# One PSUM pool for both stages of the odd mixer, the projections taking turns in the second stage's banks

## The chip, the cores and the metric

The kernel runs on one core of one Trainium2 chip. A core has several engines, each with an instruction queue of its own: TensorE (PE) for matmuls and transposes, VectorE (DVE), ScalarE (ACT) and GpSimd (POOL) for everything elementwise, and SyncE (SP), which here only issues DMAs. Matmuls write to PSUM, which has eight banks of 128 x 512 float32. The metric is the device time of one execution in microseconds (us); a smaller number is better.

## The reference

The program is a diffusion trunk of two layers over 256 latent and 256 context tokens, 1024 wide, in float32. Each layer is a mixer, modulated by a conditioning vector (adaLN), and then a mixture of 32 experts. The change is in the mixer of the second ("odd") layer, which joins a bidirectional gated DeltaNet (GDN, 4 heads of 128) with multi-head latent attention (MLA, 8 heads). Cut to what matters:

```
h = modulate(rms_norm(x), shift, scale)          # 512 tokens x 1024
q, k, v, z, tail = split(h @ odd_w_in)            # 4 x 512 columns, and 432: gates, MLA q rank 256, kv rank 128, rope 32
q, k, v = silu(short_conv5(.))                    # 5 taps along the tokens
q, k = l2_norm(q), l2_norm(k)
beta = sigmoid(tail[0:8]);  log_a = -exp(a_log) * softplus(tail[8:16] + dt_bias)
# GDN, in chunks, forward and backward in time:
T = strict_lower(beta * (k k^T) * gamma) + I      # gamma: decays from cumsum(log_a)
u, w = solve(T, beta v), solve(T, beta k exp(g))
o, S = scan over chunks of (u - w S, ...)
# MLA: q from rms_norm(cq) @ wq_up, k and v from rms_norm(ckv) @ wkv_up, rope, softmax attention
y = concat(rms_norm(o) * silu(z), attention) @ odd_w_out
x = x + gate * y;  x = x + gate2 * experts(modulate(rms_norm(x)))
```

The vectors shift, scale and gate come from silu(c) @ ada_w + ada_b, called "ada" in the kernel; it is computed in pieces of 2048 columns that are slipped in between other work.

## The kernel before, in words

The order of the instructions on each engine is not the order of the source. The odd mixer is built under a scheduler that has its own model of how long things take, and that emits on each engine what it thinks can start first; which buffers a pool has is part of what it sees, so a change of a pool can reorder every queue. The experts behind it have a hand-written PE order.

`odd_mixer` (L1341 to L1579) has two stages, each with a PSUM pool of its own, and the second pool opens when the first has closed.

Stage 1, pool `odps`: 4 banks named acc, 2 named mx, 2 named g. It normalises and transposes the tokens (L792); projects k (`proj_T`, the three matmuls L128 to L130 of a product of numbers split in a high and a low half); runs the 5-tap convolution of k on DVE (L1477, 4 taps by 4 heads) with, for each head, column sums of squares (L1485) and k k^T (L1494) on PE; projects the 432 tail columns (`tail_proj`, four banks, one for 128 tokens each: g, g, acc, acc); makes the gates, the decays (`gdn_decays`, L1586 on DVE, L1588 on PE, an Exp on ACT at L1591) and the matrices Ball (L1456, 32 multiplications on DVE); solves the 32 x 32 diagonal blocks on DVE (`gdn_solve`, L1630 to L1659); projects q, z and v; and, only after the solve (`issue_after`), convolves q and v on DVE (L1477 again), with the sums for q (L1485, copied to rq by L1487). The tail's MLA ranks are normed (L1337) and transposed (L1433, L1437), k is transposed to rows (L1507, into k_tok) and v too (L1500, into v_tok).

Stage 2, pool `gdps`: 2 banks named at, 3 mx, 2 mx2, 1 po. Inverses by doubling (`gdn_inverse`, L1672 to L1688) for the chunks 2 and 3 run interleaved with MLA's up projections (L1855) and their norms; then the second ada group (called ada2 here: L700 into po, copied to ada_r at L703, written to DRAM by L707 and read back as f1A by L734), which needs nine pieces of weights (one of them the bias row); then the chunks 0 and 1, the scans and the attention.

Weights come in by SP through five buffers named w (L110). Before each projection a piece of w is split: ACT writes the high half wh (L120) and DVE the low half wl (L121), with two buffers of each. SP issues in order; an SP instruction that waits for a buffer holds up the ones behind it.

Of the kernel before, what the change touches and what calls it, by code (L numbers as in the profile page):

```python
# [58 lines left out]
class Trunk:  # L59
# [1280 lines left out]
    def odd_mixer(self, ada, x_sb, x_done, S):  # L1340
# [23 lines left out]
        hp = xst.enter_context(tc.tile_pool(reuse_waits="tile", name="odh", bufs=1, side="right"))  # L1364
        psum = xst.enter_context(tc.tile_pool(reuse_waits="tile", name="odps", bufs=1, space=PSUM))
        hT = [hp.tile([128, 8, 512], F32R, name=f"hT{i}") for i in range(2)]
        with tc.tile_pool(reuse_waits="tile", name="odx", bufs=1) as xp:
            chunk = self.norm_T([x_sb[:, t] for t in range(NT)], hT, xp, lambda i: psum.tile(
                [128, 2, 256], F32, name="mx" if i in (4, 5) else "acc", bufs=2 if i in (4, 5) else 4),
                lambda c2: self.mods[1], 7)  # L1370
            for c2 in range(4):
                chunk(c2)
# [4 lines left out]
        cw = pool.tile([128, 12, 5], F32, name="cw")  # L1377
        pc = psum.tile([128, 12, 8], F32, name="mx", bufs=2)
        for a in range(12):
# [14 lines left out]

        def acc():
            return psum.tile([128, 512], F32, name="acc", bufs=4)

        dec = pool.tile([128, 2, NT, 4], F32, name="dec")
        tl = pool.tile([128, NT, 432], F32, name="tl")

        def tail_proj():
            names = iter(("g", "g", "acc", "acc"))

            def bank():
                n = next(names)
                return psum.tile([128, 512], F32, name=n, bufs=2 if n == "g" else 4)

            pa = self.proj_blocks(hT, S["tail"], range(NT), bank, 432)
            for t in range(NT):
                nc.scalar.activation(tl[:, t], pa[t][:, 0:432], AF.Copy)  # L1410
# [16 lines left out]
        def tail():  # L1427
            nc.vector.tensor_copy(kr, tl[:, :, 400:432])
            for t in range(NT):
                ps = tl[:, t]  # L1430
                ck = self.rms_rows(ps[:, 272:400], kvnw, 128, pool, "ckn")
                pt = psum.tile([128, 4, 128], F32, name="mx", bufs=2)
                nc.tensor.transpose(pt[:, 0], ck, self.ident)  # L1433
                if t < 2:
                    cq = self.rms_rows(ps[:, 16:272], qnw, 256, pool, "cqn")
                    for c in range(2):
                        nc.tensor.transpose(pt[:, 1 + c], cq[:, c * 128:(c + 1) * 128], self.ident)  # L1437
                    nc.scalar.activation(cqT[:, :, t * 128:(t + 1) * 128], pt[:, 1:3], AF.Copy)
                nc.scalar.activation(ckvT[:, t * 128:(t + 1) * 128], pt[:, 0], AF.Copy)
# [19 lines left out]
        def conv(kind, w0, pa):  # L1459
# [3 lines left out]
            for h in range(4):  # L1463
# [16 lines left out]
                if kind != "v":  # L1480
                    sq = raw.rearrange("p a b -> p (a b)")
                    nc.scalar.activation(sq, s, AF.Square)
                    ss = psum.tile([128, 4], F32, name="mx", bufs=2)[:, :nt]
                    for t in range(nt):
# [5 lines left out]
                    nc.vector.tensor_scalar_add(r, ss, 1e-6)  # L1490
                    kk = psum.tile([128, 4, 128], F32, name="mx", bufs=2)
                    for t in range(4):
# [4 lines left out]
                    continue  # L1497
                pt = psum.tile([128, 4, 128], F32, name="mx", bufs=2)
                for t in range(nt):
# [3 lines left out]
        def k_rows():  # L1503
            for h in range(4):
                pt = psum.tile([128, 4, 128], F32, name="mx", bufs=2)
                for t in range(4):
                    nc.tensor.transpose(pt[:, t], kT[:, h, t * 128:(t + 1) * 128], self.ident)  # L1507
                nc.scalar.activation(k_tok[:, :, h], pt, AF.Copy)
# [29 lines left out]
        gst.close()  # L1538
        with tc.tile_pool(reuse_waits="tile", name="gd2", bufs=1, side="right") as p2, tc.tile_pool(reuse_waits="tile", name="mla", bufs=1) as mp, \
                tc.tile_pool(reuse_waits="tile", name="gdps", bufs=1, space=PSUM) as psum:  # L1540
            mqT = mp.tile([96, 8, 256], F32, name="mqT")
# [24 lines left out]
            with tc.tile_pool(reuse_waits="tile", name="mla2", bufs=1) as p1:  # L1566
# [9 lines left out]
                for _ in att:  # L1576
                    pass
        return [(g[:, c, 0:256], g[:, c, 256:512]) for c in range(4)] + \
            [tuple(x[c // 2][:, c % 2] for x in attT) for c in range(4)], held  # L1579

    def decay(self, lhs, msk, lacol, pool, psum, g, ps, rl):
# [3 lines left out]
        for h in range(4):  # L1585
            nc.vector.tensor_scalar(r[:, 128 * h:128 * h + 128], f32(msk), lacol[:, h:h + 1], None, op0=OP.mult)  # L1586
        ps = psum.tile([128, 512], F32, name=ps[0], bufs=2)
        nc.tensor.matmul(ps, f32(lhs), r, start=True, stop=True)  # L1588
# [5 lines left out]
    def gdn_decays(self, la, Ball, tri, keep, pool, psum):  # L1594
        nc = self.nc
        U, L, Us, Ls = tri
        ones = self.ones
        pe = psum.tile([128, 2, 3, 16], F32, name="g", bufs=2)
        for d, (a, b) in enumerate(((U, Ls), (L, Us))):
# [5 lines left out]
        for t in (2, 3, 0, 1):  # L1605
            for d, (lhs, msk) in enumerate(((Ls, U), (L, Us))):
                self.decay(lhs, msk, la[:, d, t], pool, psum, Ball[:, d, t], ("mx" if d else "g", 4), "cv")
        return ee, la
# [547 lines left out]
```

## Time and profile before

| | |
|---|---|
| times of three runs | 1827.74, 1832.84, 1834.61 us, median 1832.84 |
| the profiled execution | 1832.54 us, of which the span of the trace is 1830.7 |
| PE busy | 1698.1 us (93% of the span), mean granted clock 0.959 |
| DVE, ACT, POOL busy | 854.9, 434.9, 352.7 us |
| the odd mixer in the span | about 1007 (first transposes) to 1296 us; stage 2 from 1158 |
| the odd layer's experts | to the end of the span, PE and DMA both full from 1400 on |

The trace gives, for each engine, every instruction with its start and length in us from the span's start, and behind it in brackets how long the engine sat idle before and which engine's write released it. "clk" or PEclk is the clock granted to PE, as a share of full speed. Where several equal instructions follow each other a row has their count (x4) and the length of the group.

### The profile page before, as it was taken

How to read it: one execution, taken by the hardware profiler on the slowest of the kernel's cores; microseconds unless marked ns; L12 is line 12 of the kernel's file. 1: busy time of each engine (PE TensorE's matmuls, PEld its weight loads, DVE VectorE, ACT ScalarE, POOL GpSimd, SP SyncE). 2: the span in 40 equal slices, each digit the busy share in tenths (PEclk: the TensorE clock that was granted, in tenths of full speed). 3: DMA queues.
4: the chain of work that ended last, by engine and by line, in shares of the span. 5: the costliest groups of instructions: out<-in, count | busy, mean ns of one | idle time of the engine just before them, and what ended most of it. 6: DMA issues, size and time to landing. Idle time of an engine off the chain costs nothing. (4 is left out here: it accounts for less than half of the span.)

```text
span 1830.7 us, 22058 instructions
## 1 busy us (share of the span) xinstructions
PE 1698.1 (93%) x8722; PEld 986.4 (54%) x8722; DVE 854.9 (47%) x1621; ACT 434.9 (24%) x698; POOL 352.7 (19%) x313
## 2 busy tenths in 40 slices
PE   6999988986999999999987998899879999999997
PEld 4767677765454444444432775588743444434442
DVE  3336158776334434344345679576353332333222
ACT  2335245441111111101101573443410000000000
POOL 2102055241112212122122110232310110101010
PEclk9999999987989999999998999899969999999999
DMA  8655521234878999999995335510569999999996
GB/s 297 233 216 205 220 114 38 105 119 180 354 322 321 392 392 394 397 397 391 397 390 186 99 115 195 195 60 1 160 280 406 415 418 415 417 416 418 416 416 281
DMA packets 115674, 511.79 MB, mean 280 GB/s; under 512 B 16254, under 2 KB 26434, under 8 KB 77031
## 3 DMA queue, kind: packets, MB, share of 16 engines
q1 hardware_dynamic: 115564, 510.31, 71.1%
q8 instruction: 71, 1.16, 0.3%
q14 instruction: 39, 0.32, 0.0%
HBM read 508.09 MB, written 2.18 MB: 279 GB/s over the span
## 5 line engine op out<-in xcount | busy, mean ns | idle before, releaser
L313 PE MATMUL gu<-wx,xT 128*64 128x512 f32 x640 | 292.8, 601 | 1.1 <-DMA wx<-moe_w_up_in 0.8
L312 PE MATMUL gu<-w,xT 128*64 128x512 f32 x568 | 263.6, 606 | 0.0
L312 PE MATMUL gu<-wx,xT 128*64 128x512 f32 x472 | 215.9, 599 | 0.0
L347 PE MATMUL y<-wx,aT 128*64 128x512 f32 x648 | 179.7, 615 | 12.1 <-DVE aT L333 9.0
L313 PE MATMUL gu<-w,xT 128*64 128x512 f32 x400 | 183.8, 603 | 0.6 <-SPq L599 0.5
L376 POOL TENSOR_TENSOR x_sb<-x_sb,tm 128x512 f32<-128x512 f32 x64 | 99.0, 1546 | 390.2 <-DVE tm L375 390.2
L316 ACT ACTIVATE sg<-gu 64x512 f32<-64x512 f32 x65 | 38.5, 593 | 556.5 <-PE gu L313 556.5
L375 DVE TENSOR_TENSOR tm<-sc,mx 128x512 f32<-128x512 f32 x128 | 85.5, 689 | 155.5 <-PE sc L371 153.8
L312 PEld LDWEIGHTS gu<-w,xT 128*64 128x64 f32 x568 | 72.8, 138 | 122.6 <-issue 119.1
L347 PE MATMUL y<-w,aT 128*64 128x512 f32 x392 | 120.0, 609 | 10.2 <-DVE aT L333 7.6
L265 PE MATMUL xg<-gt,h2h 128*128 128x256 f32 (+1 forms) x416 | 116.7, 314 | 10.7 <-DVE xT L273 6.0
L121 DVE TENSOR_TENSOR wl<-w,wh 128x1024 fp32r<-128x1024 f32 (+1 forms) x64 | 81.7, 1280 | 84.4 <-ACT wh L120 83.8
L265 PE MATMUL xg<-gt,h2l 128*128 128x256 f32 (+1 forms) x416 | 109.9, 297 | 0.0
L347 PEld LDWEIGHTS y<-wx,aT 128*64 128x64 f32 x648 | 54.4, 141 | 94.2 <-issue 74.6
L265 PEld LDWEIGHTS xg<-gt,h2h 128*128 128x128 f32 x416 | 85.8, 206 | 34.8 <-DVE tm L356 10.5
L313 PEld LDWEIGHTS gu<-wx,xT 128*64 128x64 f32 x640 | 81.9, 137 | 41.7 <-issue 24.0
L120 ACT ACTIVATE wh<-w 128x1024 fp32r<-128x1024 f32 (+1 forms) x72 | 74.8, 1046 | 122.7 <-PE acc L130 85.9
L312 PEld LDWEIGHTS gu<-wx,xT 128*64 128x64 f32 x472 | 59.7, 136 | 78.9 <-issue 73.3
L370 PE MATMUL sc<-yh,S 128*128 128x512 f32 (+1 forms) x194 | 87.3, 450 | 4.9 <-DVE tm L375 3.1
L382 DVE TENSOR_TENSOR x_sb<-x_sb,sc 128x512 f32<-128x512 f32 x66 | 43.9, 685 | 98.5 <-PE sc L371 98.1
L129 PE MATMUL acc<-wl,hT 128*128 128x512 f32 (+1 forms) x224 | 88.8, 396 | 0.2 <-DVE wl L121 0.2
L128 PE MATMUL acc<-wh,hT 128*128 128x512 f32 (+1 forms) x224 | 87.3, 403 | 0.0
(649 smaller groups left out, 3082.3 us busy)
## 6 DMA issues: line engine op xcount, KB each, us to landing
wx<-moe_w_down_in SPq DMA_DIRECT2D x81, 1024.0 KB, 10.9
wx<-moe_w_up_in SPq DMA_DIRECT2D x80, 1024.0 KB, 14.4
w<-moe_w_gate_in SPq DMA_DIRECT2D x71, 1024.0 KB, 7.6
wx<-moe_w_gate_in SPq DMA_DIRECT2D x59, 1024.0 KB, 15.4
w<-moe_w_up_in SPq DMA_DIRECT2D x50, 1024.0 KB, 11.3
w<-moe_w_down_in SPq DMA_DIRECT2D x49, 1024.0 KB, 10.3
w<-ada_w_in SPq DMA_DIRECT2D x48, 1024.0 KB, 6.7
w<-even_w_in_in SPq DMA_DIRECT2D x14, 1024.0 KB, 8.5
```

Source lines behind the costliest of these rows:

```text
L120: nc.scalar.activation(hv, src, AF.Copy)
L121: self.lo_eng[0].tensor_tensor(lv, src, f32(hv), op=OP.subtract)
L128: mm(ps, a[0], b[0], start=start, stop=False)
L129: mm(ps, a[0], b[1], start=False, stop=False)
L265: nc.tensor.matmul(ps[:, k], src[:, t, c0 + k, :], gt[t], start=(i == 0), stop=(i == 2 * NT - 1))
L312: nc.tensor.matmul(g, xs[:, c, :], G[c // 4][:, c % 4, :], start=(c == 0), stop=(c == 7))
L313: nc.tensor.matmul(v, xs[:, c, :], U[c // 4][:, c % 4, :], start=(c == 0), stop=(c == 7))
L347: nc.tensor.matmul(y[h][r], u["aT"][:, c, r], W()[j][2][cc][:, c % 2, 512 * h:512 * h + 512], start=(c == 0), stop=(c == 3))
L370: nc.tensor.matmul(p, s, yh[:M], start=True, stop=False)
L375: nc.vector.tensor_mul(tm, p, mx5[t // 2][:, 512 * h:512 * h + 512])
L376: (nc.gpsimd if h else nc.vector).tensor_add(xv, xv, tm)
L382: nc.vector.tensor_add(xv, xv, p)
```

## The change

The first pool and the second become one, `odps` with the second's banks (at 2, mx 3, mx2 2, po 1), open for the whole mixer. In stage 1, `acc()` hands out banks of mx2 and at in turns; the tail's four banks are po, mx, mx2 and at; the decays' g (two banks) becomes po (one bank); mx has three banks and no longer two. Nothing that is computed changes.

```diff
-        psum = xst.enter_context(tc.tile_pool(reuse_waits="tile", name="odps", bufs=1, space=PSUM))
+        pst = ExitStack()
+        psum = pst.enter_context(tc.tile_pool(reuse_waits="tile", name="odps", bufs=1, space=PSUM))
+        turns = [0]
+
+        def acc():
+            turns[0] += 1
+            return psum.tile([128, 512], F32, name=("at", "mx2")[turns[0] % 2], bufs=2)
+
...
-        def acc():
-            return psum.tile([128, 512], F32, name="acc", bufs=4)
-
...
-            names = iter(("g", "g", "acc", "acc"))
+            names = iter((("po", 1), ("mx", 3), ("mx2", 2), ("at", 2)))
...
-                pt = psum.tile([128, 4, 128], F32, name="mx", bufs=2)
+                pt = psum.tile([128, 4, 128], F32, name="mx", bufs=3)
...
-        with tc.tile_pool(reuse_waits="tile", name="gd2", bufs=1, side="right") as p2, tc.tile_pool(reuse_waits="tile", name="mla", bufs=1) as mp, \
-                tc.tile_pool(reuse_waits="tile", name="gdps", bufs=1, space=PSUM) as psum:
+        with tc.tile_pool(reuse_waits="tile", name="gd2", bufs=1, side="right") as p2, tc.tile_pool(reuse_waits="tile", name="mla", bufs=1) as mp:
...
+        pst.close()
...
-        ps = psum.tile([128, 512], F32, name=ps[0], bufs=2)
+        ps = psum.tile([128, 512], F32, name=ps[0], bufs={"mx": 3, "mx2": 2, "po": 1}[ps[0]])
...
-        pe = psum.tile([128, 2, 3, 16], F32, name="g", bufs=2)
+        pe = psum.tile([128, 2, 3, 16], F32, name="po", bufs=1)
...
-                self.decay(lhs, msk, la[:, d, t], pool, psum, Ball[:, d, t], ("mx" if d else "g", 4), "cv")
+                self.decay(lhs, msk, la[:, d, t], pool, psum, Ball[:, d, t], ("mx" if d else "po", 4), "cv")
```

(Lines of the kernel after are four higher from L1405 or so on: L1485 is L1489, L1494 is L1498, L1477 is L1481, L1433 is L1437, L1672 is L1676.)

The change of the pool reorders the queues at three places that matter here. First PE in the tail projection. Before, its 96 matmuls (128x432, into g and acc) run on, and the sums of squares and k k^T of a head of k (into mx) are slipped in between where they come ready:

```order
L128 MATMUL g<-wh,hT_7605 128x432 x2
L128 MATMUL acc<-wh,hT_7605 128x432 x2
L1485 MATMUL mx<-o_ones,raw 128x1 x4
L1494 MATMUL mx<-okT 128x128 x4
L129 MATMUL g<-wl,hT_7605 128x432
L130 MATMUL g<-wh,hT_7606 128x432
L128 MATMUL g<-wh,hT_7605 128x432
```

After, at the same place, the sums and k k^T of all four heads stand together in the middle of the tail projection:

```order
L130 MATMUL at<-wh,hT_7606 128x432
L1489 MATMUL mx<-o_ones,raw 128x1 x4
L1498 MATMUL mx<-okT 128x128 x4
L1489 MATMUL mx<-o_ones,raw 128x1 x4
L1498 MATMUL mx<-okT 128x128 x4
L1489 MATMUL mx<-o_ones,raw 128x1 x4
L1498 MATMUL mx<-okT 128x128 x4
L1489 MATMUL mx<-o_ones,raw 128x1 x4
L1498 MATMUL mx<-okT 128x128 x4
L128 MATMUL mx<-wh,hT_7605 128x432
L129 MATMUL mx<-wl,hT_7605 128x432
L130 MATMUL mx<-wh,hT_7606 128x432
```

Ahead of them stand 36 of the tail's matmuls, in the banks po, mx2 (mx_7980) and at; behind them the 12 first ones of its mx bank, which comes in the rotation of mx behind the heads' sums and k k^T, and then the other 48. On ACT the third and fourth split of the tail's weights (L120) stand behind the four copies of k k^T.

Second PE where the first stage ends. Before, the v projection's last matmul is followed by the sums for q, the transposes of stage 1 and the first inverses; ada2 (L700) comes behind 12 of these:

```order
L130 MATMUL acc<-hT_7605,wl 128x512
L1485 MATMUL mx<-o_ones,raw 128x1 x8
L1433 MATMUL mx<-c_ident,ckn 128x128
L1437 MATMUL mx<-c_ident,cqn 128x128 x2
L1433 MATMUL mx<-c_ident,ckn 128x128
L1437 MATMUL mx<-c_ident,cqn 128x128 x2
L1433 MATMUL mx<-c_ident,ckn 128x128 x2
L1507 MATMUL mx<-c_ident,okT 128x128 x16
L1500 MATMUL mx<-c_ident,cv 128x128 x16
L1672 MATMUL mx<-c_ident,iX 128x128 x12
L700 MATMUL po<-w,k_ones_row 32x512 x4
L700 MATMUL po<-w,k_silu_c 32x512 x8
```

After, all of ada2 stands directly behind the v projection, with the sums for q between its last pieces:

```order
L130 MATMUL mx_8647<-hT_7605,wl 128x512
L700 MATMUL po<-w,k_ones_row 32x512 x4
L700 MATMUL po<-w,k_silu_c 32x512 x24
L1489 MATMUL mx<-o_ones,raw 128x1 x2
L700 MATMUL po<-w,k_silu_c 32x512 x4
L1489 MATMUL mx<-o_ones,raw 128x1 x6
L700 MATMUL po<-w,k_silu_c 32x512 x4
L1437 MATMUL mx<-c_ident,ckn 128x128
L1441 MATMUL mx<-c_ident,cqn 128x128 x2
L1437 MATMUL mx<-c_ident,ckn 128x128
```

So ada2 has moved ahead of the end of stage 1, and with it, on SP, its weight loads and the write and read back of ada_r: the loads of MLA's norm weights and rope table (qkw, rope), which were issued ahead of six of ada2's loads, now stand behind all of it and behind three of the loads of odd_w_out. The last sums for q use the bank of mx that the first ones had, and wait for its copy (L1491) on DVE.

Third DVE at the end of the convolutions of q and v. Before, the small instructions for q's norm and for the last two blocks of MLA's kv rank (cknr, ckn) lie between the taps:

```order
L626 TENSOR_SCALAR rq<-rq 128x8
L1477 SCALAR_TENSOR_TENSOR cv<-acc,cw,cv 128x2x254
L626 TENSOR_SCALAR cknr<-ckns 128x1
L1477 SCALAR_TENSOR_TENSOR cv<-acc,cw,cv 128x2x254
L1337 SCALAR_TENSOR_TENSOR ckn<-tl,cknr,kvnw 128x128
L1477 SCALAR_TENSOR_TENSOR cv<-acc,cw,cv 128x2x254
L1536 TENSOR_SCALAR rq<-rq 128x8
L1337 SCALAR_TENSOR_TENSOR ckn<-tl,cknr,kvnw 128x128
```

After, they stand behind the last tap, and with them the copy of ada2's result:

```order
L1481 SCALAR_TENSOR_TENSOR cv<-mx_8647,cw,cv 128x2x254
L1491 COPY rq<-mx 128x2 x4
L626 TENSOR_SCALAR rq<-rq 128x8
L703 COPY ada_r<-po 128x512
L1540 TENSOR_SCALAR rq<-rq 128x8
L626 TENSOR_SCALAR cknr<-ckns 128x1
L1337 SCALAR_TENSOR_TENSOR ckn<-tl,cknr,kvnw 128x128
L626 TENSOR_SCALAR cknr<-ckns 128x1
L1337 SCALAR_TENSOR_TENSOR ckn<-tl,cknr,kvnw 128x128
```

Elsewhere on DVE, one split of q's weights (L121) that stood between the decays of L1586 now stands ahead of the first of them, and the split that stood between the taps of q now stands ahead of the solve's last steps. From the scans on, the order of the engines is nearly the same in both kernels, and the experts' is the same.

## Rows read from the trace of the kernel before

**Rows 1.** The head of the profile's page: the span and the busy time of each engine.
```profile
span 1830.7 us, 22058 instructions
PE 1698.1 (93%) x8722; PEld 986.4 (54%) x8722; DVE 854.9 (47%) x1621; ACT 434.9 (24%) x698; POOL 352.7 (19%) x313
```

**Rows 2.** The view by windows, of stretches of the odd mixer: after the stretch its length, then the busy time and instruction count of PE, PE's weight loads, DVE, ACT and POOL, the granted clock, the DMA share and GB/s.
```profile
1040.00:1064.00 24.00, 24.00 (x145) 23.10 (x144) 15.11 (x28) 14.36 (x28) 2.14 (x4) 1.00 0.14 45
...
1100.00:1140.00 40.00, 34.25 (x156) 23.50 (x156) 37.97 (x62) 10.59 (x19) 1.80 (x2) 0.91 0.53 202
1140.00:1158.00 18.00, 10.19 (x48) 7.88 (x49) 12.87 (x31) 11.81 (x26) 6.46 (x8) 0.62 0.05 10
1158.00:1198.00 40.00, 39.56 (x274) 26.18 (x273) 22.80 (x52) 15.79 (x27) 10.76 (x11) 1.00 0.71 264
1198.00:1240.00 42.00, 41.78 (x332) 37.59 (x330) 30.07 (x51) 19.75 (x37) 15.00 (x14) 1.00 0.08 26
1240.00:1296.00 56.00, 52.35 (x365) 43.44 (x364) 36.70 (x68) 22.52 (x47) 13.45 (x10) 0.97 0.07 22
```

**Rows 3.** The same view, of the experts of the odd layer.
```profile
1400.00:1800.00 400.00, 391.52 (x1718) 167.23 (x1712) 127.00 (x224) 33.63 (x55) 37.74 (x40) 1.00 1.02 416
```

**Rows 4.** PE's timeline in the tail projection: the first of its matmuls, the start of one head's sums and k k^T and the first matmul behind them, the projection's last matmul, and the first matmul behind it. The columns are start, length, engine, line, operation, tiles and shape.
```profile
1039.88 0.56 PE L128 MATMUL g<-wh,hT 128*128 128x432 f32 x2
...
1050.14 0.95 PE L1485 MATMUL mx<-o_ones,raw 128*128 128x1 f32 x8
...
1051.85 0.44 PE L129 MATMUL g<-wl,hT 128*128 128x432 f32 x1
...
1063.91 0.44 PE L130 MATMUL acc<-wh,hT 128*128 128x432 f32 x1
1064.19 0.28 PE L128 MATMUL acc<-hT,wh 128*128 128x256 f32 x1
```

**Rows 5.** ACT's timeline: a split of the tail's weights, and the squares of the last head of k.
```profile
1049.56 0.93 ACT L120 ACTIVATE wh<-w 128x864 fp32r<-128x864 f32 x1 [2.62 <-PE acc L130]
...
1053.60 0.64 ACT L1482 ACTIVATE raw<-okT 128x512 f32<-128x512 f32 x1
```

**Rows 6.** DVE's timeline from the first decays over the solve to the end of the convolutions.
```profile
1070.36 0.88 DVE L1586 TENSOR_SCALAR cv<-o_U,la 128x128 f32<-128x128 f32 x4
...
1092.74 2.05 DVE L1635 STREAM_TRANSPOSE sys<-prd 128x1024 f32<-128x1024 f32 x1 [0.88 <-ACT prd L1632]
...
1128.42 1.58 DVE L1477 SCALAR_TENSOR_TENSOR oqT<-raw,cw,oqT 128x254 f32<-128x254 f32 x4
1129.93 1.21 DVE L121 TENSOR_TENSOR wl<-w,wh 128x1024 fp32r<-128x1024 f32 x1
...
1136.77 1.53 DVE L1477 SCALAR_TENSOR_TENSOR cv<-acc,cw,cv 128x508 f32<-128x508 f32 x2 [0.89 <-ACT cv L1474]
...
1150.12 0.73 DVE L1477 SCALAR_TENSOR_TENSOR cv<-acc,cw,cv 128x508 f32<-128x508 f32 x1
...
1150.85 0.35 DVE L1337 SCALAR_TENSOR_TENSOR ckn<-tl,cknr,kvnw 128x128 f32<-128x128 f32 x1
```

**Rows 7.** POOL's timeline: the powers for the norms of q and of a block of the kv rank.
```profile
1148.66 1.65 POOL L627 TENSOR_TENSOR rq<-rq,k_mhalf 128x8 f32<-128x8 f32 x1
1150.27 0.55 POOL L627 TENSOR_TENSOR cknr<-cknr,k_mhalf 128x1 f32<-128x1 f32 x1
```

**Rows 8.** PE's timeline at the end of stage 1: the last matmul of the v projection, two waits, the transposes of k, and the first inverse of stage 2.
```profile
1137.67 0.40 PE L130 MATMUL acc<-hT,wl 128*128 128x512 f32 x1
...
1141.59 0.58 PE L1485 MATMUL mx<-o_ones,raw 128*128 128x1 f32 x4 [2.73 <-DVE rq L1487]
...
1151.35 0.45 PE L1433 MATMUL mx<-c_ident,ckn 128*128 128x128 f32 x1 [0.55 <-DVE ckn L1337]
1151.59 3.72 PE L1507 MATMUL mx<-c_ident,okT 128*128 128x128 f32 x16
...
1158.02 0.60 PE L1672 MATMUL mx<-c_ident,iX 128*128 128x128 f32 x4
```

**Rows 9.** ada2: its matmuls as one group (the view of line L700 in stage 2, with their lengths and first and last start), a run of 16 of them in PE's timeline and what follows it, and the copy of the result on DVE.
```profile
L700 PE MATMUL po<-w,k_silu_c x64: 592/592/617, 1161.0 to 1189.1; 128*32 128x512 f32 x64
...
1161.05 1.92 PE L700 MATMUL po<-w,k_silu_c 128*32 128x512 f32 x16
1162.90 0.66 PE L1672 MATMUL mx<-c_ident,iX 128*128 128x128 f32 x4
...
1189.74 0.69 DVE L703 COPY ada_r<-po 128x512 f32<-128x512 f32 x1 [0.78 <-PE po L700]
```

**Rows 10.** SP: its timeline (issue of MLA's norm weights, of six loads of ada2, of the write of ada_r and the read back as f1A), one row of the view of waits (us in total, times, longest), and one of the DMA view (KB each, median us to landing).
```profile
1138.93 0.33 SPq L1831 DMA_DIRECT2D qkw<-mla_qk_norm_q_in  x1
...
1161.18 16.52 SPq L110 DMA_DIRECT2D w<-ada_w_in  x6
...
1190.46 1.03 SPq L707 DMA_DIRECT2D ada<-ada_r  x2
1196.72 0.34 SPq L734 DMA_DIRECT2D f1A<-ada  x1
...
SPq L110 <- PE po L700: 35.1, 9, 20.9
...
w<-ada_w_in SPq DMA_DIRECT2D x16, 1024.0 KB, 6.6
```

More of the change, by code (lines that the diff above doesn't have):

```diff
@@ L1368, in odd_mixer @@
             chunk = self.norm_T([x_sb[:, t] for t in range(NT)], hT, xp, lambda i: psum.tile(
-                [128, 2, 256], F32, name="mx" if i in (4, 5) else "acc", bufs=2 if i in (4, 5) else 4),
+                [128, 2, 256], F32, name="mx", bufs=3) if i in (4, 5) else acc().rearrange("p (a b) -> p a b", a=2),
                 lambda c2: self.mods[1], 7)
@@ L1377, in odd_mixer @@
         cw = pool.tile([128, 12, 5], F32, name="cw")
-        pc = psum.tile([128, 12, 8], F32, name="mx", bufs=2)
+        pc = psum.tile([128, 12, 8], F32, name="mx", bufs=3)
         for a in range(12):
@@ L1401, in tail_proj @@
         def tail_proj():
-            names = iter(("g", "g", "acc", "acc"))
+            names = iter((("po", 1), ("mx", 3), ("mx2", 2), ("at", 2)))
             def bank():
-                n = next(names)
-                return psum.tile([128, 512], F32, name=n, bufs=2 if n == "g" else 4)
+                n, b = next(names)
+                return psum.tile([128, 512], F32, name=n, bufs=b)
             pa = self.proj_blocks(hT, S["tail"], range(NT), bank, 432)
@@ L1482, in conv @@
                     nc.scalar.activation(sq, s, AF.Square)
-                    ss = psum.tile([128, 4], F32, name="mx", bufs=2)[:, :nt]
+                    ss = psum.tile([128, 4], F32, name="mx", bufs=3)[:, :nt]
                     for t in range(nt):
@@ L1490, in conv @@
                     nc.vector.tensor_scalar_add(r, ss, 1e-6)
-                    kk = psum.tile([128, 4, 128], F32, name="mx", bufs=2)
+                    kk = psum.tile([128, 4, 128], F32, name="mx", bufs=3)
                     for t in range(4):
@@ L1497, in conv @@
                     continue
-                pt = psum.tile([128, 4, 128], F32, name="mx", bufs=2)
+                pt = psum.tile([128, 4, 128], F32, name="mx", bufs=3)
                 for t in range(nt):
@@ L1504, in k_rows @@
             for h in range(4):
-                pt = psum.tile([128, 4, 128], F32, name="mx", bufs=2)
+                pt = psum.tile([128, 4, 128], F32, name="mx", bufs=3)
                 for t in range(4):
```

## The prediction

> **What bounds the kernel now.** I read the head of the page first. PE is busy 1698.1 of the span's 1830.7 us [rows 1], so only stretches in which PE stands idle or runs at a low clock have much to give, and work that adds to PE's queue elsewhere costs its full length. The view by windows says where those stretches are. In the odd mixer PE is full in the tail projection (24.00 of 24 us), nearly idle between 1140 and 1158 (10.19 of 18 us busy, clock 0.62) and full again from 1158 on (39.56 of 40, then 41.78 of 42) [rows 2]. What holds PE in the idle stretch is DVE: it is busy 37.97 of 40 us from 1100 to 1140 [rows 2], first with the solve and then with the convolutions of q and v, and PE's last transposes of stage 1 wait for it (2.73 us for rq, then ckn) [rows 8]. So the mixer's start to 1158 is set by a chain on DVE: end of the tail projection, gates, decays, solve (its last write feeds the taps that start at 1128.42), convolutions (last tap from 1150.12), last ckn at 1150.85 [rows 6], then PE's transposes and the first inverse at 1158.02 [rows 8]. From there PE's own work is the bound. The experts behind the mixer are full on PE (391.52 of 400 us) and on DMA (share 1.02) [rows 3]; they begin with a stretch of routing that depends on the mixer, so a shift of the mixer's end should move the program's end one for one.
>
> The profiled execution took 1832.54 us, 1.8 more than its span; the median of the three runs is 1832.84, so the sum below is made against 1832.54 and needs no correction. Their spread is 6.9 us, and 0.5% of the time, 9.2 us, is about what can be told from no change.
>
> **The change, part by part.** No instruction's work changes. What counts is the order.
>
> *The tail projection, later.* Before, 96 matmuls and three heads' groups fill 1039.88 to 1064.19; a group takes 1.71 us (1050.14 to 1051.85), which leaves (24.31 - 5.1) / 96 = 0.20 us for a matmul [rows 4]. After, 36 of them end at 1039.9 + 7.2 = 1047.1; then PE must take all four heads, and the last head's squares start on ACT at 1053.60 and end at 1054.2 [rows 5]. With its group PE is at 1055.9, and the other 60 matmuls take 12.0: 1067.9, or +3.7. The split of the tail's weights that they need (0.93 on ACT [rows 5], as much on DVE) can only start when 6 of the 12 first ones are done, and lies beside the other 6 and the next four, which need the high half only; I cost it at nothing, and 1 us if that cover fails. The bounds of this part are 0 (conv k's splits move off DVE and the heads come ready earlier) and +7.
>
> *Splits on DVE.* One split of q's weights now stands ahead of the decays: 1.21 by the other split of that shape [rows 6], so the decays start at +4.9. The same number of splits (nine) lies between the decays and the solve's end in both orders, but the one that stood in front of the copies for the first transpose no longer covers ACT's part of these: its 0.88 us of idle [rows 6] grows by a split, +1.2. The solve ends at +6.1, 1134.5 for the taps' start. The convolutions then get shorter: 22.4 us before (1128.42 to 1150.85), less a split of 1.21, less 0.89 of idle [rows 6] that the later start covers, less about 1.0 of small instructions that now stand behind them: 19.3, end near 1153.8, +3.
>
> *The end of stage 1.* Behind the last tap stand now in a row: the first copy for rq, the last sums for q on PE (which wait for its bank), their copy, four matmuls of ada2, the copy ada_r (0.69 [rows 9]), and twice cknr, a power on POOL (0.55, and 1.65 for rq in front [rows 7]) and ckn (0.35 [rows 6]). That is 0.7 us from the last tap's start to the last ckn before, and with some 0.3 us for each of the steps without a row I make it 4.6 us from the last tap's end to the last transpose of ckn, so 1158.4 against 1151.35 [rows 8]. k's and v's transposes keep their 6.7 us (1151.35 to 1158.02), and the first inverse comes at 1165.0: **+7.0 us**. As bounds I take +2 (the tail's delay caught up, and the small instructions overlapping) and +12.
>
> *ada2, out of the full stretch.* The 72 matmuls of ada2 (64 and the bias row's 8) lie between 1160 and 1189.7 in a stretch where PE is full [rows 2, 9]; 16 of them hold PE 1.85 us (1161.05 to 1162.90), 0.116 each, and the groups of 8 just under 1.0, so all take 8.3 to 9.0 us. They move into the idle stretch. The v projection's last split moves from 1129.93 [rows 6] to a place ahead of the solve's last steps, near 1126 as I count back from 1134.5, and frees the buffers that ada2's first loads need; its end comes about 6 us earlier than the 1137.7 of before [rows 8], at 1131.5, where ada2 can begin. Nine pieces go through three buffers (the other two hold MLA's weights), so in three batches from 1126 on; a load lands after 6.6 us in the median [rows 10], and with three in flight I take 8.5 for a batch: the last is used near 1151.5, 2.3 us before the last tap. So there they are hidden. In stage 2 DVE is busy only 22.80 of 40 us and ACT 15.79 [rows 2], so they can follow a PE that has less to do, but the inverses are a chain of PE and DVE and some of the freed time will be waits: bounds 0 and 9.0, and I take **-7.5**, close to the row of the full PE.
>
> *MLA's small loads.* qkw and rope were issued at 1138.93, now behind ada_r's write and read back. The read back was issued 6.3 us after the write (1190.46, 1196.72 [rows 10]); with ada_r copied near 1155.9, qkw goes out near 1162.7 and is used near 1168. Its cost is nothing with some 2 us to spare, and up to 3 without.
>
> *po with one bank, mx with three.* The decays' matmuls alternate between po and mx, and only every second one needs po's single bank; DVE's four multiplications for each [rows 6] set the pace. Nothing.
>
> Sum: 1832.54 + 7.0 - 7.5 = **1832.0 us**.
>
> On the banks themselves the trace shows PE full with short groups in the tail projection at a granted clock of 1.00 [rows 2]. The Trainium skill, in "Perfetto Trace Analysis", section "Matmuls", advises that independent groups rotate through different banks so that the eviction of one overlaps the next; by this rule an alternation of at and mx2 costs nothing against four acc banks, and the sum stays where it is, as the rotation is kept with four banks.
>
> **The rivals.**
>
> *A. Stage 2 does not shorten.* The inverses' chains (PE to DVE and back) and not PE's queue set its end. For it: from 1240 on PE is busy only 52.35 of 56 us [rows 2], which are waits. Against it: 41.78 of 42 before that. Then 1832.5 + 7.0 = 1839.5.
>
> *B. ada2's weights come late (slower).* ada2 stands at the head of PE's queue, ahead of the sums for q, k's transposes and the inverses, and PE takes its queue in order. Its loads wait for buffers; SP waited 35.1 us for L700 in nine waits, and six loads took 16.52 us to issue [rows 10]. At the pace of before, 29.6 us from the first matmul to the copy (1160.1 to 1189.7 [rows 9]), it would end near 1161 when it starts at 1131.5. It decides from the point where its last load lands behind the last tap, 1153.8. Then the first inverse starts at about +11.3, and qkw behind ada_r is late as well, so that the gain of 7.5 is lost: 1832.5 + 11.3 = 1844.
>
> *C. The delay is smaller than I make it.* ACT and DVE lose the splits in front of conv k's heads, the tail catches up, and the whole of 9.0 is won: 1832.5 + 2 - 9 = 1825.5. For it: DVE is busy only 15.11 of 24 us in the tail [rows 2].
>
> *D. The clock falls in the tail projection.* PE waits between the heads' groups from 1047 to 1055. In the idle stretch before, with 10.19 of 18 us busy, the mean granted clock was 0.62 [rows 2], which is mostly the lower level of 1.2 GHz. If the 60 matmuls behind the wait went at that level, half of them or all, they would take 6 to 12 us more: 1838 to 1844, and 1841 as the middle. The Trainium skill names such a case in "TensorE: Matmul & The Clock Gate", section "A second HAM failure mode: psum-queue depth-cycling": short idle times of PE between groups that cycle through PSUM let its clock go up and down. By that rule D is what happens; against it the tail of before, which cycles through its banks too, holds 1.00 [rows 2].
>
> **How the numbers follow.** I give the forecast 0.40, A 0.18, B 0.12, C 0.20, D 0.10. The predicted time is the forecast's. Its own range, from the terms' nearer bounds, is 1827 to 1838. The range for 8 in 10 reaches to C below and to B above with some play: 1822 to 1846. Faster than 1823.7 (0.5%): half of C and a little of the forecast, 0.13. Slower than 1842.0: two thirds of B, a third of D and a part of A with a longer delay, 0.17. The rest, 0.70, is no change.
>
> **What would show it.** In the profile after: the first projection of q behind the tail near 1068 (before 1064.19); the taps of q from about 1134.5; the last L1437 near 1158.4 and the first L1676 near 1165.0; the copy ada_r near 1155 and no L700 behind the first inverse; the granted clock of the idle stretch higher than 0.62; and the mixer's end where it was, within a microsecond or two. B is right if PE waits on a DMA at L700 when the taps are done; A if PE's busy share in the 40 us behind the first inverse falls well below 39.56; D if the clock between 1050 and 1068 is under 1.00. I am wrong altogether if the end of stage 1 is not later.

## The result, and the profile after

The changed kernel takes 1845.72 us (median of 4 runs, 1845.58 to 1846.34), beside 1830.57 for the kernel before: 0.8% slower, ratio 1.0082 with a 95% interval of 1.0059 to 1.0105. The predicted time was 1832.0.

The head of the page after the change:

```profile
span 1844.4 us, 22056 instructions
PE 1709.6 (93%) x8722; PEld 995.2 (54%) x8722; DVE 858.1 (47%) x1621; ACT 435.8 (24%) x698; POOL 353.6 (19%) x313
```

The instructions are the same, as many matmuls as in [rows 1], but PE is busy for 11.5 us more: the same matmuls took longer. So PE's busy time does not count work alone; it grows when the granted clock falls. The view by windows of the tail projection shows where more than half of it was (length, busy time and count of PE, PE's loads, DVE, ACT, POOL, granted clock, DMA share, GB/s):

```profile
1036.00:1046.00 10.00, 10.00 (x49) 9.04 (x49) 8.96 (x13) 7.59 (x12) 0.00 (x0) 1.00 0.28 86
1046.00:1050.00 4.00, 2.28 (x19) 2.06 (x19) 2.87 (x6) 2.43 (x5) 0.00 (x0) 1.00 0.13 51
1050.00:1064.00 14.00, 14.00 (x60) 13.67 (x61) 1.48 (x5) 4.21 (x7) 2.91 (x1) 0.51 0.00 0
1064.00:1074.00 10.00, 10.00 (x53) 9.46 (x52) 3.88 (x8) 4.87 (x14) 1.10 (x3) 1.00 0.01 2
```

PE is full up to 1046, idle for 1.7 of the next 4 us, and then full again for 14 us, at a granted clock of 0.51, the level of 1.2 GHz. Before, the whole stretch ran at 1.00 [rows 2]. The busy column alone shows nothing of it; the clock column and the count do (60 matmuls in 14 us, before 145 in 24 [rows 2]). PE's timeline of the same place:

```profile
1047.02 1.14 PE L1498 MATMUL mx<-okT 128*128 128x128 f32 x8
1049.88 1.50 PE L1489 MATMUL mx<-o_ones,raw 128*128 128x1 f32 x8 [1.72 <-ACT raw L1486]
1051.24 2.06 PE L1498 MATMUL mx<-okT 128*128 128x128 f32 x8
...
1059.77 0.71 PE L128 MATMUL mx<-wh,hT 128*128 128x432 f32 x1
...
1061.00 0.56 PE L128 MATMUL mx<-wh,hT 128*128 128x432 f32 x1
1061.36 0.56 PE L129 MATMUL mx<-wl,hT 128*128 128x432 f32 x1
...
1064.13 0.36 PE L128 MATMUL po<-wh,hT 128*128 128x432 f32 x1
...
1073.67 0.28 PE L128 MATMUL mx<-hT,wh 128*128 128x256 f32 x1
```

Behind the 36 matmuls of the tail and the first head, PE waits 1.72 us for the second head's squares. Then k k^T of a head takes 2.06 us for 1.14, a matmul of the tail starts every 0.36 us (1061.00 to 1061.36) where it was 0.20 [rows 4], and q's projection starts at 1073.67 where it started at 1064.19 (some 1.8 us of that is the fourth head's group, which before lay within q's projection).

On DVE, from the first decay to the last ckn (columns as in [rows 6], which these rows answer to):

```profile
1079.91 1.23 DVE L121 TENSOR_TENSOR wl<-w,wh 128x1024 fp32r<-128x1024 f32 x1 [0.27 <-ACT wh L120]
1081.05 0.87 DVE L1590 TENSOR_SCALAR cv<-o_U,la 128x128 f32<-128x128 f32 x4
...
1098.05 1.14 DVE L1460 SCALAR_TENSOR_TENSOR Ball<-kks,bt,Ball 128x128 f32<-128x128 f32 x4 [0.84 <-ACT Ball L1595]
1100.54 1.14 DVE L1460 SCALAR_TENSOR_TENSOR Ball<-kks,bt,Ball 128x128 f32<-128x128 f32 x4 [1.36 <-ACT Ball L1595]
1105.38 1.23 DVE L121 TENSOR_TENSOR wl<-w,wh 128x1024 fp32r<-128x1024 f32 x1 [3.70 <-ACT wh L120]
...
1111.89 2.06 DVE L1639 STREAM_TRANSPOSE sys<-prd 128x1024 f32<-128x1024 f32 x1 [2.02 <-ACT prd L1636]
...
1146.09 3.65 DVE L1481 SCALAR_TENSOR_TENSOR oqT<-raw,cw,oqT 128x254 f32<-128x254 f32 x4
...
1166.20 0.73 DVE L1481 SCALAR_TENSOR_TENSOR cv<-mx,cw,cv 128x508 f32<-128x508 f32 x1
...
1173.72 0.35 DVE L1337 SCALAR_TENSOR_TENSOR ckn<-tl,cknr,kvnw 128x128 f32<-128x128 f32 x1 [0.73 <-POOL cknr L627]
```

Three idle times of 0.84, 1.36 and 3.70 us stand in front of Ball's multiplications and a split; before there was none. They wait for ACT, and ACT waits for PE. The first two wait for an Exp of a late decay; the third is in front of a split, whose half on ACT waits for a projection's matmul, and the last Exp comes only behind that. The last decay's matmul starts 20.3 us behind the first (1083.77 to 1104.09), before it was 11.6. PE's timeline and ACT's tell why. PE:

```profile
1089.44 1.02 PE L1592 MATMUL po<-cv,o_Ls 128*128 128x512 f32 x2
...
1096.25 1.12 PE L1592 MATMUL po<-cv,o_Ls 128*128 128x512 f32 x2
...
1104.09 1.02 PE L1592 MATMUL po<-cv,o_Ls 128*128 128x512 f32 x2
```

ACT:

```profile
1090.49 0.60 ACT L1595 ACTIVATE Ball<-po 128x512 f32<-128x512 f32 x1
...
1097.42 0.60 ACT L1595 ACTIVATE Ball<-po 128x512 f32<-128x512 f32 x1 [1.97 <-PE po L1592]
...
1104.29 1.06 ACT L120 ACTIVATE wh<-w 128x1024 fp32r<-128x1024 f32 x1 [3.78 <-PE at L130]
1105.25 0.58 ACT L1595 ACTIVATE Ball<-po 128x512 f32<-128x512 f32 x1
```

The bank po is read out by 1091.1, and the next decay in it runs at 1096.25, with no idle time of PE in front of it: PE was at work on other things in its queue. So it isn't the bank that holds the decay up on the chip: its place in PE's queue is behind pieces of the z projection and of the first ada group. That the number of banks open to the decays decides this place is what e2 and e7 below show; how the scheduler came to it was not looked at.

At the end of stage 1, PE's timeline (the answer to [rows 8]):

```profile
1163.43 1.01 PE L1489 MATMUL mx<-o_ones,raw 128*128 128x1 f32 x4 [2.61 <-ACT raw L1486]
1164.37 1.93 PE L700 MATMUL po<-w,k_silu_c 128*32 128x512 f32 x8
1166.24 2.72 PE L1489 MATMUL mx<-o_ones,raw 128*128 128x1 f32 x12
1168.89 1.93 PE L700 MATMUL po<-w,k_silu_c 128*32 128x512 f32 x8
...
1174.21 0.45 PE L1437 MATMUL mx<-c_ident,ckn 128*128 128x128 f32 x1 [0.76 <-DVE ckn L1337]
1174.46 3.62 PE L1511 MATMUL mx<-c_ident,okT 128*128 128x128 f32 x16
...
1180.67 2.20 PE L1676 MATMUL mx<-c_ident,iX 128*128 128x128 f32 x16
```

ada2 is done before the last transposes, as its order says; eight of its matmuls take 1.93 us here where 16 took 1.92 in the full stretch [rows 9], again the lower clock. The view by windows has it at 0.50:

```profile
1165.00:1175.00 10.00, 8.55 (x39) 4.97 (x32) 4.35 (x14) 4.92 (x16) 2.74 (x3) 0.50 0.70 247
```

The last ckn is transposed at 1174.21, 7.3 us behind the last tap, and the first inverse starts at 1180.67: 22.7 us later than before.

From there to the span's end it is 1844.4 - 1180.67 = 663.7 us, before it was 1830.7 - 1158.02 = 672.7 [rows 1, 8]. So stage 2 gives 9.0 us back, and 13.7 us of difference between the spans are left.

The following table is the same reading for all kernels of this study: the length of each part in us, from the starts in PE's and DVE's timelines, and the span less the first inverse. The parts matter more than the sum, since the stretch ahead of the odd mixer, which no kernel here changes, varied by up to 9.1 us between the profiled executions (its end lay between 998.0 and 1007.1).

| kernel | first transposes to q's projection | to first decay | to first tap of q | to last transpose of ckn | to first inverse | sum, stage 1 | to the span's end |
|---|---|---|---|---|---|---|---|
| before | 57.4 | 6.2 | 58.1 | 22.9 | 6.7 | 151.2 | 672.7 |
| after | 66.6 | 7.4 | 65.0 | 28.1 | 6.5 | 173.6 | 663.7 |
| e1, tail banks | 58.1 | 5.8 | 64.9 | 27.3 | 4.1 | 160.1 | 663.4 |
| e2, decays in mx | 65.3 | 7.4 | 59.2 | 24.0 | 5.1 | 160.9 | 662.7 |
| e12, both | 58.1 | 5.8 | 59.7 | 26.9 | 4.0 | 154.4 | 662.8 |
| e5, filler | 61.9 | 7.4 | 65.5 | 24.9 | 7.3 | 167.0 | 667.7 |
| e3, before with ada2 moved | 57.3 | 6.2 | 58.1 | 26.5 | 6.9 | 154.9 | 662.9 |
| e4, ada2 put back | 66.5 | 7.4 | 65.0 | 25.1 | 6.8 | 170.7 | 673.5 |
| e6, both and ckn | 58.1 | 6.1 | 59.9 | 24.2 | 5.4 | 153.7 | 662.9 |
| e7, before with one g | 57.3 | 6.2 | 66.8 | 22.6 | 7.7 | 160.5 | 670.2 |

One of e7's ten executions took 4707.81 us; the median given for e7 below is over all ten (1838.24 without that one), and its ratio leaves it out.

### The profile page after: what moved, and what is told of

Read it like the earlier page. It is cut to its first block, busy times and chain, and to the rows that moved or that the text cites. A ratio compares the mean times of both kernels' runs of the same rounds, so it can differ in the third digit from the quotient of the medians.

```text
span 1844.4 us, 22056 instructions
## 1 busy us (share of the span) xinstructions
PE 1709.6 (93%) x8722; PEld 995.2 (54%) x8722; DVE 858.1 (47%) x1621; ACT 435.8 (24%) x698; POOL 353.6 (19%) x313
## 5 line engine op out<-in xcount | busy, mean ns | idle before, releaser
L375 DVE TENSOR_TENSOR tm<-sc,mx 128x512 f32<-128x512 f32 x128 | 85.6, 689 | 155.4 <-PE sc L371 153.7
L121 DVE TENSOR_TENSOR wl<-w,wh 128x1024 fp32r<-128x1024 f32 (+1 forms) x64 | 82.0, 1282 | 96.2 <-ACT wh L120 95.6
L313 PEld LDWEIGHTS gu<-wx,xT 128*64 128x64 f32 x640 | 81.9, 137 | 42.6 <-issue 25.1
L120 ACT ACTIVATE wh<-w 128x1024 fp32r<-128x1024 f32 (+1 forms) x72 | 74.8, 1046 | 126.9 <-PE acc L130 79.5
L312 PEld LDWEIGHTS gu<-wx,xT 128*64 128x64 f32 x472 | 59.7, 136 | 77.7 <-issue 72.2
L265 PEld LDWEIGHTS xg<-gt,h2l 128*128 128x128 f32 x416 | 86.5, 208 | 0.0
L370 PEld LDWEIGHTS sc<-yh,S 128*128 128x128 f32 (+1 forms) x194 | 36.3, 187 | 87.4 <-issue 73.0
```

The lines of the kernel that those rows point to most:

```text
L120: nc.scalar.activation(hv, src, AF.Copy)
L121: self.lo_eng[0].tensor_tensor(lv, src, f32(hv), op=OP.subtract)
L265: nc.tensor.matmul(ps[:, k], src[:, t, c0 + k, :], gt[t], start=(i == 0), stop=(i == 2 * NT - 1))
L312: nc.tensor.matmul(g, xs[:, c, :], G[c // 4][:, c % 4, :], start=(c == 0), stop=(c == 7))
L313: nc.tensor.matmul(v, xs[:, c, :], U[c // 4][:, c % 4, :], start=(c == 0), stop=(c == 7))
L370: nc.tensor.matmul(p, s, yh[:M], start=True, stop=False)
```

## The experiments

Each is timed against the kernel before on the same chip; that kernel had medians of 1831.38, 1831.77 and 1830.53 us beside the three sets of runs (e1, e2, e12 and e5; e3, e4 and e6; e7).

**e1: the tail's banks.** The loss in the tail, without touching the decays.

```diff
-            names = iter((("po", 1), ("mx", 3), ("mx2", 2), ("at", 2)))
+            names = iter((("po", 1), ("at", 2), ("mx2", 2), ("at", 2)))
```

> The changed kernel, with the tail projection's four banks po, at, mx2, at, none of them from mx. Theory (the tail's mx bank puts all four heads' groups in a row, PE stands idle in front of the second, and the clock falls to 1.2 GHz until 1063.9): the groups lie between the tail's matmuls again, the granted clock from 1040 to 1070 is 1.00 and not 0.77, the first projection of q starts near 1064 to 1066 and not at 1073.7, and the time falls by 8 to 9 us, to about 1837. Rival (the single bank po in the decays costs the time): the tail is faster, but the solve ends where it did within 2 us, and the time stays near 1844. Open: whether the late decays (DVE idle 5.9 us in front of its Ball multiplications) go with it.

Measured: 1831.20 us, ratio to before 1.0001 (0.9989 to 1.0013). This edit alone takes back nearly all the loss, some 14 us and not 8 to 9. With no tail bank taken from mx, 48 matmuls of the tail stand ahead of the first head and the groups lie between the others. PE's windows (length, busy, clock, DMA share, GB/s):

```profile
1036.00:1046.00 10.00, 10.00 (x53) 1.00 0.32 107
1046.00:1052.00 6.00, 6.00 (x49) 1.00 0.00 1
1052.00:1063.00 11.00, 11.00 (x71) 1.00 0.01 1
```

PE is full and the clock stays at 1.00. The table says where the rest is: 8.5 us in the tail, 1.6 in front of the decays, and 2.4 in the last transposes. The decays stay late (64.9 us): they are a loss of their own and do not come from the tail.

**e2: the decays in mx.**

```diff
-                self.decay(lhs, msk, la[:, d, t], pool, psum, Ball[:, d, t], ("mx" if d else "po", 4), "cv")
+                self.decay(lhs, msk, la[:, d, t], pool, psum, Ball[:, d, t], ("mx", 4), "cv")
```

> The changed kernel, with all eight decays in mx (three banks) and none in po (one bank). Theory (the single bank lets the scheduler put the last decays behind the z projection, and DVE waits for them): the last Exp comes within 13 us of the first decay on DVE and not 19, the 5.9 us that DVE idles between the Ball multiplications go, and the time falls by 5 to 7 us, to 1839 to 1841; the tail projection stays slow, with the clock at 0.77. Rival (the tail alone makes the loss, the decays are only late behind it): no change within 2 us of 1845.7.

Measured: 1831.08 us, ratio 0.9999 (0.9983 to 1.0016). The part that it aims at falls as expected, from 65.0 to 59.2 us, and the last decay's matmul starts 13.1 us behind the first and no longer 20.3 (the last Exp comes 16.0 us behind the first decay on DVE, for 24.2 in the changed kernel; the expectation had 13 and 19). But the whole gain, 14.6 us, is twice what was expected. Of the rest, 4.1 us lie between the first tap and the last ckn and 1.4 behind it (the pieces of ada2 stand otherwise there), 1.0 in stage 2, and 1.3 in the tail, whose order is the same: PE waits the same 1.72 us there and its clock falls too, to 0.57 in a window of 12 us, but comes back about 11 us behind the wait and not 14. Why these parts fell is not shown.

**e12: both.** Both diffs above.

> Both edits: the tail's banks po, at, mx2, at, and all decays in mx. Theory (the two losses are separate and add, and the second ada group stays out of stage 2): 14 to 16 us less than the changed kernel, 1830 to 1832, with stage 2 starting near 1165 and still 9 us shorter than in the kernel before. If one of the two edits removes both losses, it is no faster than that one alone. If the early place of the second ada group costs more than it brings (rival), it stays above 1835.

Measured: 1823.32 us, ratio 0.9964 (0.9947 to 0.9981): faster than the kernel before. It is also less than the 1830 to 1832 expected, which counted e1 and e2 at their expected gains. The two losses are separate, each in its part: tail 58.1 as in e1, decays 59.7 as in e2. In the whole they do not add (14.5 and 14.6 us alone, 22.4 together): what e2 won between the taps and the last ckn, 4.1 us, is 1.2 here. What is left of the change is ada2's move, 9.9 us won in stage 2 for 3.2 lost in stage 1.

**e5: a filler in front of the second head.** Does the low clock cost the time, or does it only go with PE's wait? Four matmuls of 128x512 are added where PE waits; their result is overwritten.

```diff
                     kk = psum.tile([128, 4, 128], F32, name="mx", bufs=3)
+                    if h == 0:
+                        for _ in range(4):
+                            nc.tensor.matmul(kk.rearrange("p a b -> p (a b)"), kT[:, h, 0:128], kT[:, h], start=True, stop=True)
```

> The changed kernel with four extra 128x512 matmuls on the first head's k (their result is overwritten) between the first head's sums and its k k^T, about 3.4 us of PE work in the 1.7 us of idle in front of the second head's sums. Theory (the fallen clock is most of what the tail loses): the granted clock stays at 1.00 from 1046 to 1070, the heads' groups take 1.7 us and not 3.4, the first projection of q starts some 5 us earlier than 1073.7 in spite of the extra work, and the time falls by 4 to 6 us, to about 1841. Rival (PE's wait for the heads is what counts, and the clock only shows it): the time rises by up to 3 us.

Measured: 1842.21 us, ratio 1.0071 (1.0045 to 1.0096), 3.5 us less than the changed kernel. The tail says it plainly. PE's windows (the first is the filler, the second the heads' groups and the tail's matmuls behind them):

```profile
1037.00:1041.00 4.00, 4.00 (x17) 2.42 (x16) 2.88 (x6) 3.13 (x6) 0.00 (x0) 1.00 0.11 41
1041.00:1053.00 12.00, 11.96 (x83) 10.87 (x82) 2.87 (x6) 4.56 (x7) 2.91 (x1) 1.00 0.00 1
```

With more work for PE the part up to q's projection is 4.7 us shorter (61.9 for 66.6): the clock stays at 1.00 through the same four groups in a row, and from the second head's sums to q's projection it takes 17.65 us for 23.79. So it is the clock that costs the tail its time. The filler takes away the idle time and also puts large matmuls among the small ones; which of the two keeps the clock up is not separated. A part of the gain is lost elsewhere: this kernel's order has the router's weights behind other loads on SP, and PE waits for them behind the mixer. The view of waits, of that stretch (total, times, longest):

```profile
PE rl L1262 <- DMA rw<-router_expert_w_in: 3.7, 1, 3.7
```

The changed kernel has no such wait. By the parts of the table the filler is 2.6 us shorter than the changed kernel, and without this wait it would be 6.3. The four executions spread from 1834.64, the profiled one, to 1845.83, so the parts say more here than the median.

**e3: the kernel before, with ada2 alone moved.** The two pools stay; ada2 goes into a bank of g at the end of stage 1.

```diff
+        for a, w in S["ada2"]:
+            self.ada_mm(*a, w, ada, lambda: psum.tile([128, 512], F32, name="g", bufs=2), self.cpool)
         self.rsqrt(rq, rq, 1)
...
-                for a, w in S["ada2"]:
-                    self.ada_mm(*a, w, ada, lambda: psum.tile([128, 512], F32, name="po", bufs=1), self.cpool)
```

> The kernel before with its two pools, and ada2 alone moved: its matmuls go to a bank of g at the end of stage 1. Theory (ada2 out of stage 2 is worth its own 9 us, whatever the pools are): from the first inverse to the span's end 663 us and not 672.7; stage 1 keeps its 151 us or loses up to 5 to the pieces of ada2 between the last transposes; 1822 to 1827 in all. Rival (the one pool is what shortens stage 2, since its banks need no hand-over): the rest stays at 672 and the time does not fall, or rises by what stage 1 loses.

Measured: 1828.55 us, ratio 0.9987 (0.9976 to 0.9998). Stage 2 shortens by 9.8 us, so it is ada2's move and not the single pool that does it. Stage 1 loses 3.7 us, the last transposes and ada2's pieces between them, and of the difference of 6.1 us in these parts 3.2 are seen in the medians: a gain, but a smaller one than expected.

**e4: the changed kernel, with ada2 put back.** An extra transpose into its bank, overwritten, makes it wait for v_tok.

```diff
+                def late():
+                    t = psum.tile([128, 512], F32, name="po", bufs=1)
+                    nc.tensor.transpose(t[:, 0:128], v_tok[:, 0, 3], self.ident)
+                    return t
+
                 for a, w in S["ada2"]:
-                    self.ada_mm(*a, w, ada, lambda: psum.tile([128, 512], F32, name="po", bufs=1), self.cpool)
+                    self.ada_mm(*a, w, ada, late, self.cpool)
```

> The changed kernel with ada2 put back: one extra transpose of v_tok into its bank (overwritten) holds its matmuls behind v's last transposes. Theory (ada2's move wins 9 us in stage 2, and its place in PE's queue costs some of the 7 us behind the last tap): from the first inverse to the end 672 us again and not 663.7, the last transpose of ckn 2 to 4 us behind the last tap and not 7.3; 4 to 7 us slower than the changed kernel, 1850 to 1853. Rival (ada2 at the head of PE's queue is what makes the changed kernel slow): the time falls below 1840.

Measured: 1852.38 us, ratio 1.0114 (1.0099 to 1.0129), 6.7 us slower than the changed kernel. From the first inverse to the end it is 673.5 us again (1.7 of it is a wait of PE for the router's weights, which the changed kernel does not have), and the part from the taps to the last ckn is 3.0 us shorter. So ada2's early place wins 8 to 10 us and costs 3, and it isn't what makes the changed kernel slow.

**e6: both edits, and four buffers for ckn.** Can the row of small instructions behind the taps be taken away too?

```diff
-        y = pool.tile([128, n], F32, name=name, bufs=2)
-        ss = pool.tile([128, 1], F32, name=name + "s", bufs=2)
+        nb = 4 if name == "ckn" else 2
+        y = pool.tile([128, n], F32, name=name, bufs=nb)
+        ss = pool.tile([128, 1], F32, name=name + "s", bufs=nb)
...
-        r = pool.tile([128, 1], F32, name=name + "r", bufs=2)
+        r = pool.tile([128, 1], F32, name=name + "r", bufs=nb)
```

> The kernel with both edits (tail banks po, at, mx2, at; decays in mx) and four buffers for ckn and its sums where there were two. Theory (the third and fourth block's norms wait for PE to transpose the first two, which stand behind ada2 in PE's queue): all four ckn are written before the convolutions of q and v, the last transpose of ckn comes 1 to 3 us behind the last tap and not 7.3, and the time is 4 to 5 us below that of both edits, 1818 to 1820. Rival (the row of small instructions behind the taps is set by rq and ada_r, not by ckn): no change within 2 us.

Measured: 1823.02 us, ratio 0.9952 (0.9940 to 0.9964): the fastest kernel here, but no different from e12 (1823.32). The rival's forecast of no change holds, though not by its reason. All four ckn are written early (the last on DVE at 1074.40), and yet PE's last transpose of one comes 3.7 us behind the last tap's end at 1150.6 (1 to 3 expected, 7.3 in e12), since pieces of ada2 stand in front:

```profile
1147.91 1.01 PE L1490 MATMUL mx<-o_ones,raw 128*128 128x1 f32 x4
1148.85 1.93 PE L700 MATMUL po<-w,k_silu_c 128*32 128x512 f32 x8
...
1152.40 1.94 PE L700 MATMUL po<-w,k_silu_c 128*32 128x512 f32 x8
1154.27 0.48 PE L1438 MATMUL mx<-c_ident,ckn 128*128 128x128 f32 x1
...
1159.67 2.29 PE L1677 MATMUL mx<-c_ident,iX 128*128 128x128 f32 x16
```

With ckn out of the way, ada2 at the lower clock (1.93 us for eight) and its order set the place. The part up to the last ckn is 2.7 us shorter than in e12, but eight more of ada2 now stand behind it, and the taps came 0.5 us later: the sum of stage 1 falls by 0.7.

**e7: the kernel before, with one bank for the decays.** The cross-check of e2: the other bank of g, now gx, serves the tail alone.

```diff
-            names = iter(("g", "g", "acc", "acc"))
+            names = iter(("g", "gx", "acc", "acc"))
...
-                return psum.tile([128, 512], F32, name=n, bufs=2 if n == "g" else 4)
+                return psum.tile([128, 512], F32, name=n, bufs=4 if n == "acc" else 1)
...
-        ps = psum.tile([128, 512], F32, name=ps[0], bufs=2)
+        ps = psum.tile([128, 512], F32, name=ps[0], bufs=1 if ps[0] == "g" else 2)
...
-        pe = psum.tile([128, 2, 3, 16], F32, name="g", bufs=2)
+        pe = psum.tile([128, 2, 3, 16], F32, name="g", bufs=1)
```

> The kernel before with one bank of g for the sums and the decays (the other bank, gx, serves the tail projection only), everything else as it was. Theory (one bank for every second decay is enough to make the decays late, without the change of pools and without a slower tail): the tail ends where it did, and from the first decay on DVE to the first tap of q it takes 64 to 65 us and not 58; stage 1 is 6 us longer, and the time rises by 5 to 7 us, to 1836 to 1838. Rival (the decays are late because the tail projection is): no change within 2 us.

Measured: 1838.56 us, ratio 1.0044 (1.0025 to 1.0062). The tail ends where it did, and from the first decay to the first tap it takes 66.8 us for 58.1 (64 to 65 expected). The last decay's matmul starts 18.7 us behind the first, before it was 11.6. DVE waits for the late Exp, as in the changed kernel:

```profile
1091.78 1.14 DVE L1456 SCALAR_TENSOR_TENSOR Ball<-kks,bt,Ball 128x128 f32<-128x128 f32 x4 [2.98 <-ACT Ball L1591]
...
1097.09 2.05 DVE L1635 STREAM_TRANSPOSE sys<-prd 128x1024 f32<-128x1024 f32 x1 [2.02 <-ACT prd L1632]
```

One bank for every second decay is enough to make the decays late, with two pools and a tail at full speed. Not all of the 8.7 us is that wait: the longer wait for prd (2.02 for 0.88 [rows 6]) also stands in e2 and e12, where no decay is late, and the new order has one more split there and three waits of DVE of 0.65 to 1.18 us.

## Why the prediction was wrong

The forecast was no change, 1832.0, from +7.0 in stage 1 and -7.5 in stage 2. Measured are +22.4 and -9.0 in the parts of the table. The places were right: the tail, the splits, the row behind the taps and ada2. The sizes of stage 1 were not. It came out 15.4 us over the forecast: 5.5 in the tail and 5.8 in the decays, which are the two steps that failed, and some 4.2 at the convolutions' end and behind it.

- *The tail projection, later: +3.7.* Measured +9.2. The order did what was read from it: 36 matmuls, four groups in a row, 60 matmuls. The term priced the 60 at 0.20 us and the groups at 1.71, the prices of a full clock. At the lower clock the three groups from 1049.88 to 1059.77 took 9.9 us for 5.1, and 12 matmuls 4.3 us (to 1064.13) for 2.4: 6.7 us together. That was rival D, with 6 to 12 us and a chance of 0.10; its sign, a clock under 1.00 between 1050 and 1068, came, though the low clock fell on three groups and 12 of the 60 matmuls. The time passed D's 1844 since the late decays came on top. The prediction saw the wait of PE and the low clock of another half-idle stretch [rows 2], and still put the full clock into the sum. On the Trainium skill's rule that was weighed there ("TensorE: Matmul & The Clock Gate", section "A second HAM failure mode: psum-queue depth-cycling"): the trace agrees that a short idle time of PE between groups is followed by the lower clock. Here it is a single one, of 1.72 us, and a wait for ACT's squares and not for a bank; e1, whose tail has as many banks in rotation and no such wait, stays at 1.00.
- *Splits on DVE, +4.9 at the first decay and +6.1 at the solve's end, and "po with one bank, mx with three: nothing".* The first is right on top of the tail: 7.4 us from q's projection to the first decay for 6.2. The second came too: DVE waits 2.02 us for prd where it waited 0.88 [rows 6]. The third failed. From the decays to the taps it took 7.0 us more and not 1.2, and the rest of it is DVE's idle times of 0.84, 1.36 and 3.70. The prediction took DVE's multiplications as the pace and the single bank as free in time, and on the chip the bank is indeed free. But the last decays had moved in PE's queue behind pieces of the z projection, and the prediction did not look at their place there. e2 and e7 show both directions.
- *The end of the convolutions and the row behind them.* Taps to last ckn: 28.1 us, of which 20.8 to the end of the last tap (19.3 expected) and 7.3 behind it (4.6 expected). The row was right in kind; the lower clock makes its PE steps twice as long. The forecast's sign that the clock of the idle stretch would rise above 0.62 did not come: with ada2 in it, it is 0.50 from 1165 to 1175. k's and v's transposes kept their time, as said.
- *ada2, out of the full stretch: -7.5.* Measured -9.0 here, and 9.8 in e3 and e4 (in e4 with the 1.7 of the router's weights): at least the whole of its busy time, 8.3 to 9.0. Rival A (stage 2 does not shorten) falls. Rival B (ada2's loads late) falls too: PE waited for ada2's weights between 1147 and 1159, but not behind the last tap, and e4 shows that its early place is a gain. Rival C did not come.
- *qkw and rope behind ada2, nothing.* They went out at 1176.3 and were used at 1184.50 without a wait of PE.

The bands: the range (1822 to 1846) just holds the time, but the chance of slower by over 0.5% was put at 0.17. The loss of 22.4 in stage 1 is even beyond the bound of +12 that was given for it, because the tail alone went beyond its bound of +7 and the decays had none. That the time still lies within the range is luck: the range reached so far up for rival B, which did not come.

## What to carry to other kernels

When a new order lets PE run into a short wait amid small matmuls, price what follows at the lower clock before you take the full one; a few matmuls of filler, or large matmuls between the small ones, can be cheaper than the wait. When a pool is changed under a scheduler, a bank that is free soon enough on the chip can still cost, because the number of banks changes the queue: read the order of every producer on the critical chain, not only that of the tiles that lost a bank. And split a change into its parts: here one (ada2's move) shortened stage 2 by 9 us, and two others, both one-line choices of a bank, hid it.

## What the runs showed of the hardware

A wait of 1.72 us between groups of small matmuls, behind a long full stretch, was followed by 14 us at a granted clock of 0.51 although PE was busy all the time; the same four groups in a row, with the wait filled by 128x512 matmuls, ran at 1.00. PE's full queue did not bring the clock back before about 1064, and the 6.7 us that this cost are some four times the wait itself. In e2 the same wait in the same order was followed by a shorter stretch at the lower clock, which ended about 11 us behind it.
